# Two of three branch projections as Strassen pairs in a hybrid decoder layer on one Trainium2 core

## The chip, the cores and the metric

The kernel runs on one core of a Trainium2 chip. The core's engines work side by side, each in its own order: TensorE (PE in the profile; its weight loads are PEld), VectorE (DVE), ScalarE (ACT), GpSimd (POOL) and SyncE (SP), and its DMA queues are fed by SP, POOL and ACT. The metric is the device time of one execution in microseconds, here the median of three runs.

## The reference

One mixer layer, for a prompt of 1024 tokens and 8 single-token samples, width D = 1024, all in float32:

```python
h = rmsnorm(x, norm_gain)
proj = h @ w_in                                # q, k, v, gla_g, a_lr, u, pool_g, xq, xg, merge
br_gla  = rmsnorm(gla(q, k, v, gate(a_lr)))    * silu(gla_g)
br_pool = multiscale_pool(u)                   * silu(pool_g)
br_x    = cross_attention(xq, memory)          * silu(xg)
bproj   = einsum('btnw,nwd->btnd', [br_gla, br_pool, br_x], w_branch)   # three 1024 x 1024 products
merged  = sum over n of sigmoid(merge[n]) * bproj[n]
y = rmsnorm(x + merged @ w_out)
```

The change concerns `bproj` and `merged`: three products of a [1024 x 1024] weight with a branch's [1032 tokens x 1024] output (1024 prompt tokens and 8 sample tokens), each multiplied by its gate, then summed.

## The kernel before, in words

All values lie with the channels on the 128 partitions and the 1032 tokens along the free dimension, in two halves of HT = 516, each taken in two pieces of QT = 258. A product in float32 is made of three matmuls on values split into a high and a low part (`mm3`, lines 240 to 242: high times high, low times high, high times low). `split` (lines 221 and 222; with a scale lines 224 and 225) makes the parts: ACT copies the high one, then DVE subtracts it to get the low one.

**The input projection** is a list of 40 `Pair`s (0 to 39), each 256 columns of `w_in`. A pair uses one level of Strassen's method (Winograd's form): the weights are cut into four blocks, and the tokens and input channels of h too; seven products of a combined weight block with a combined block of h replace eight. The weight combinations are made for each pair (`operands`: four DVE additions at line 301, seven splits) three products ahead (`AHEAD = 3`) of their use. The seven combinations of h ("11", "21", "t2", "t1", "t3", "22", "t4", the order of `RIGHT`) are made once, and their split parts stay in 28 of the 30 large tiles of the pool `E` (1032 elements); the other two hold a pair's results c1 and c2.

Product (i, j) is the j-th of pair i. The sequence `seq` runs (i,1), (i,2), (i,3), (i,4), (i+1,0), (i,5), (i,6). A product is 24 matmuls of 258 columns. ACT copies accumulators aside (`saved`, line 612), DVE adds pieces: line 677 after product 1, line 694 after product 4, line 703 after product 5. `finish` then sends the result to scratch memory on POOL's queue. Pairs 0 to 15 make q, k, v and so on, 16 to 27 the merge gates, 28 to 39 the branches' SiLU gates, each multiplied (lines 636 and 638) by the branch's own result, which `mixed` loads (`mix` tiles) into the ring `R` of 15 small tiles. Attention, gated linear attention and pooling run in between, up to pair 36.

**The plain stage** follows: 24 units, one for 128 columns of `w_branch` in one branch (cross, then gated linear attention, then pool: `ORDER = (2, 0, 1)`). A unit is 72 matmuls of 384 or 264 columns over 8 tiles `bh`, `bl`, which `branch_k` loads and splits. At its end DVE multiplies by the sigmoid of the merge gate (line 1508) and adds the sum so far from scratch (line 1510), and the sum goes back to scratch or, in the last branch, becomes the split operand `mg` of the output projection, which is the last stage.

PE and SP keep the order in which the program issues their work; on DVE, ACT and POOL a scheduler sets it from data dependencies and from orders written with `issue_after`. SP's queue takes loads strictly in turn: a load that waits for its tile holds those behind it.

Of the kernel before, what the change touches and what calls it, by code (L numbers as in the profile page):

```python
# [42 lines left out]
EW = 1032  # L43
EXP_LN_SET = 6
# [3 lines left out]
def trunk_kernel(ctx: ExitStack, tc: tile.TileContext,  # L48
# [65 lines left out]
    def R(shape, dt=F32, name="r"):  # L114

        return shaped(wk.tile([P, 512], dt, tag="ring", name=name, bufs=NR), shape)

    def V(shape, dt=F32, name="v"):
        return shaped(wk.tile([P, 512], dt, tag="own", name=name, bufs=4), shape)
# [68 lines left out]
    brs = [cp.tile([P, NK, NS], F32, name=f"brs{n}") for n in range(3)]  # L188
# [13 lines left out]
    acc_scr = [scratch(NK, f"acc{n}_", (P, TT)) for n in range(2)]  # L202
# [78 lines left out]
    ORDER = (2, 0, 1)  # L281

    class Pair:


        def __init__(self, src, dst, s0=None, gated=None, turned=False):
            self.src, self.dst, self.s0, self.gated, self.raw = src, dst, s0, gated, [None, None]
            self.turned = turned
# [300 lines left out]
    def operand(name, k, src):  # L589
        hi, lo = (E([2, HT], F32R, name=f"o{name}{k}{j}") for j in range(2))  # L590
        split(hi, lo, src)
        ops.setdefault(name, []).append((hi, lo))
# [12 lines left out]
    def run_product(n):  # L605
# [18 lines left out]
        def finish(t, e):  # L624
# [3 lines left out]
            if p.gated:  # L628
# [11 lines left out]
                nc.vector.tensor_tensor(t[:, :, 512:HT], t[:, :, 512:HT], ss, op=ALU.mult)  # L640
            if p.turned:
# [24 lines left out]

        if j == 0:
# [13 lines left out]
        elif j == 2:  # L681
            p.r2 = []
            for c in product(p.x, n, False):
                p.r2.append(saved(p.x, c, "r2"))
                yield
# [5 lines left out]
        elif j == 4:  # L691
            for c in product(p.x, n, False):
# [6 lines left out]
        elif j == 5:  # L699
            p.e2 = E([2, HT], name="c2")  # L700
            mixed(1)
            for c in product(p.z, n, False):
# [4 lines left out]
        else:  # L707
            for c in product(p.x, n, False):
# [92 lines left out]
    def cross_scaled(h):  # L801
        xs = wk.tile([P, 16], F32, tag="xsq", name="xsq", bufs=2).rearrange("p (i b) -> p i b", i=2)
# [528 lines left out]
    def emit(n, ahead=AHEAD):  # L1331
        prepare(n + ahead)
        if seq[n] == (28, 0):
# [102 lines left out]
    units = [(o, n, d) for o, n in enumerate(ORDER) for d in range(NK)]  # L1436
    inputs = {}

    def fetch(u):
# [10 lines left out]
        acc = None  # L1450
        if o > 0:
            acc = E([TT], name="acc")
            nc.sync.dma_start(out=acc, in_=acc_scr[o - 1][d])
        inputs[u] = w, sig, acc
# [9 lines left out]
    br.append(branch_k(ORDER[0], 7))  # L1464
# [29 lines left out]
    for u, (o, n, d) in enumerate(units):  # L1494
        if d == 0 and o:
# [3 lines left out]
        w, sig, acc = inputs.pop(u)  # L1499
        act(sig, sig, AF.Sigmoid)  # L1500
        ts = [PX() for _ in CH]
# [54 lines left out]
    for hf, order in enumerate(ORDERS):  # L1556
        for tb in order:
# [13 lines left out]
            if hf == 0:  # L1571
                x = (E([D], name="y") if tb < 8 else RAW("ys").rearrange("p a b -> p (a b)"))[:m]
                nc.sync.dma_start(out=x, in_=x_p[tb * P:(tb + 1) * P] if tb < 8 else x_s)
                rows_[tb], sums[tb] = x, wk.tile([P, 4], F32, tag="yq", name="yq", bufs=9)[:m]
# [69 lines left out]
```

## Time and profile before

| | |
|---|---|
| Median of 3 runs | 1431.19 us (1431.14 to 1432.55) |
| The profiled execution, in all | 1428.62 us |
| Its span, first to last instruction | 1426.9 us |
| Granted TensorE clock | 0.998 of full |
| PE busy | 1403.6 us (98%) |
| DVE busy | 919.8 us (64%) |
| ACT busy | 678.3 us (48%) |
| The last gated pairs without other work on PE | 20.16 us each |
| Plain stage, 24 units | 1054.40 to 1326.37 us |
| From the end of the plain stage to the end of the span | 100.5 us |

A row of groups reads: source line, engine, operation, output tile <- input tiles (with partitions x elements), count, busy time and mean ns of one, and the idle time of the engine before them with what ended it. A row of a timeline reads: start, length (both us), the instruction, and the idle time before it in brackets. Lines such as L222 are those of the kernel before; in the changed kernel the same statements stand a few lines lower (L222 is L224, L677 is L768, L694 is L787, L703 is L797).

### The profile page before, as it was taken

How to read it: one execution, taken by the hardware profiler on the slowest of the kernel's cores; microseconds unless marked ns; L12 is line 12 of the kernel's file. 1: busy time of each engine (PE TensorE's matmuls, PEld its weight loads, DVE VectorE, ACT ScalarE, POOL GpSimd, SP SyncE). 2: the span in 40 equal slices, each digit the busy share in tenths (PEclk: the TensorE clock that was granted, in tenths of full speed). 3: DMA queues.
4: the chain of work that ended last, by engine and by line, in shares of the span. 5: the costliest groups of instructions: out<-in, count | busy, mean ns of one | idle time of the engine just before them, and what ended most of it. 6: DMA issues, size and time to landing. Idle time of an engine off the chain costs nothing.

```text
span 1426.9 us, 28403 instructions
## 1 busy us (share of the span) xinstructions
PE 1403.6 (98%) x10625; PEld 1345.0 (94%) x10625; DVE 919.8 (64%) x2108; ACT 678.3 (48%) x1582; POOL 293.6 (21%) x529
## 2 busy tenths in 40 slices
PE   7999999999899999999999999999999999999998
PEld 6899999999899999999999999999999999999876
DVE  6956766857687777767765777876662534654336
ACT  6744434534566656656554545444472422333222
POOL 4154222336442222222221111110000000000000
PEclk9999999999999999999999999999999999999999
DMA  9367786877564565545444556476484687632633
GB/s 347 117 202 248 251 280 208 258 222 237 138 190 130 170 192 163 165 152 166 155 150 146 176 162 210 150 217 204 150 263 148 225 273 232 228 105 86 227 112 117
DMA packets 194197, 270.05 MB, mean 189 GB/s; under 512 B 24252, under 2 KB 144084, under 8 KB 194052
## 3 DMA queue, kind: packets, MB, share of 16 engines
q1 hardware_dynamic: 129692, 151.36, 34.1%
q0 software_dynamic: 26208, 78.94, 15.5%
q10 hardware_dynamic: 38160, 37.95, 9.6%
q8 instruction: 83, 1.36, 0.4%
q14 instruction: 54, 0.44, 0.1%
HBM read 185.84 MB, written 82.80 MB: 188 GB/s over the span
## 4 chain that ended last, share of the span: by engine, by line
PE 92%; DMA 4%; DVE 3%; ACT 1%; issue 1%; SPq 0%; POOL 0%; ACTq 0%; DVEq 0%
PE px L240 26%; PE px L241 26%; PE px L242 26%; PE pz L241 2%; PE pz L242 2%; PE pz L240 2%; DMA raw<-in_w_in_dram 2%; PE pz L461 1%; PE pz L1040 1%; PE pz L1019 1%; DMA qb<-xqs 1%; PE pz L867 1%; PE pz L1021 1%; DMA pT<-pts 0%; PE pz L1126 0%
## 5 line engine op out<-in xcount | busy, mean ns | idle before, releaser
L240 PE MATMUL px<-bh,wbh 128*128 128x384 f32 (+1 forms) x576 | 184.3, 320 | 0.0
L241 PE MATMUL px<-bl,wbh 128*128 128x384 f32 (+1 forms) x576 | 184.0, 319 | 0.0
L242 PE MATMUL px<-bh,wbl 128*128 128x384 f32 (+1 forms) x576 | 183.8, 319 | 0.0
L612 ACT ACTIVATE r<-px 128x258 f32<-128x258 f32 x240 | 90.1, 377 | 54.4 <-PE px L242 53.5
L241 PEld LDWEIGHTS px<-bl,wbh 128*128 128x128 f32 x576 | 108.3, 188 | 0.0
L242 PEld LDWEIGHTS px<-bh,wbl 128*128 128x128 f32 x576 | 108.3, 188 | 0.0
L240 PEld LDWEIGHTS px<-bh,wbh 128*128 128x128 f32 x576 | 108.3, 188 | 0.0
L240 PE MATMUL px<-o,a12h 128*128 128x258 f32 x320 | 92.0, 288 | 1.4 <-DVE c L703 1.4
L240 PE MATMUL px<-ot,s1h 128*128 128x258 f32 x320 | 93.3, 292 | 0.0
L240 PE MATMUL px<-o,s4h 128*128 128x258 f32 x320 | 92.3, 288 | 0.3 <-DVE c L694 0.3
L240 PE MATMUL px<-o,a11h 128*128 128x258 f32 x320 | 92.4, 289 | 0.0
L240 PE MATMUL px<-ot,s2h 128*128 128x258 f32 x320 | 92.3, 288 | 0.0
L240 PE MATMUL px<-ot,a22h 128*128 128x258 f32 x320 | 92.0, 288 | 0.0
L240 PE MATMUL px<-ot,s3h 128*128 128x258 f32 x320 | 91.9, 287 | 0.0
L241 PE MATMUL px<-ot,s2h 128*128 128x258 f32 x320 | 90.6, 283 | 0.5 <-DVE ot L222 0.5
L241 PE MATMUL px<-o,a11h 128*128 128x258 f32 x320 | 90.7, 283 | 0.3 <-DVE o L222 0.3
L241 PE MATMUL px<-o,s4h 128*128 128x258 f32 x320 | 90.7, 283 | 0.0
L242 PE MATMUL px<-o,a11l 128*128 128x258 f32 x320 | 90.7, 283 | 0.0
L242 PE MATMUL px<-o,s4l 128*128 128x258 f32 x320 | 90.7, 283 | 0.0
L242 PE MATMUL px<-ot,s3l 128*128 128x258 f32 x320 | 90.5, 283 | 0.0
L241 PE MATMUL px<-ot,a22h 128*128 128x258 f32 x320 | 90.4, 283 | 0.0
L242 PE MATMUL px<-ot,s1l 128*128 128x258 f32 x320 | 90.4, 282 | 0.0
(479 smaller groups left out, 4687.2 us busy)
## 6 DMA issues: line engine op xcount, KB each, us to landing
raw<-in_w_in_dram ACTq DMA_DIRECT2D x72, 512.0 KB, 4.1
msc<-c POOLq DMA_DIRECT2D x24, 516.0 KB, 4.6
brsc<-c POOLq DMA_DIRECT2D x24, 516.0 KB, 4.1
sig<-msc SPq DMA_DIRECT2D x24, 516.0 KB, 6.1
brr<-brsc SPq DMA_DIRECT2D x48, 256.0 KB, 5.5
wbr<-in_w_branch_dram SPq DMA_DIRECT2D x24, 512.0 KB, 5.9
acc<-sig POOLq DMA_DIRECT2D x16, 516.0 KB, 5.4
acc<-acc SPq DMA_DIRECT2D x16, 516.0 KB, 7.2
```

The lines of the kernel that those rows point to most:

```text
L240: nc.tensor.matmul(out, lhsT=lh, rhs=rh, start=start, stop=False, skip_group_check=more)
L241: nc.tensor.matmul(out, lhsT=lh, rhs=rl, start=False, stop=False, skip_group_check=more)
L242: nc.tensor.matmul(out, lhsT=ll, rhs=rh, start=False, stop=stop, skip_group_check=more)
L461: nc.tensor.matmul(t[:, :DV], lhsT=memT[k // 2][:, k % 2, a * P:(a + 1) * P], rhs=raw[k // 2][:, k % 2], start=k == 0, stop=k == NK - 1)
L612: nc.scalar.activation(r, acc[c][:, :QT], AF.Copy)
L867: nc.tensor.matmul(t[32 * j:32 * j + 32, :DV], lhsT=pm[:, a, 4 * i + j, :], rhs=vc[j][:, a, :], start=a == 0, stop=a == 1)
L1019: nc.tensor.matmul(t[0:64, 0:P], lhsT=ki[:, 0:64], rhs=qi, start=True, stop=True)
L1021: nc.tensor.transpose(t[:, P:2 * P], kt, ident)
L1040: nc.tensor.matmul(to, lhsT=kiqi[:, 1, cs], rhs=st, start=False, stop=True)
```

## The change

The projections of cross (n = 2) and pool (n = 1) become eight more pairs, 40 to 43 and 44 to 47. Their weights are columns of `w_branch`, and their right operands are the branch's output in place of h. The order is now `(2, 1, 0)`, one merge pair (the old pair 27) moves behind the gated ones to place 39, and the gated pairs move up by one (27 to 38).

The seven right operands change twice, at pair 39 (for cross) and at pair 43 (for pool). This turnover is spread over the products: four blocks of the branch's output come as 16 tiles `b` (12 of the ring `R`, 4 of `V`), DVE makes the four differences t1, t3, t2, t4 from them by 16 subtractions of 516 elements (line 623) during the pair before (38 and 42), and each of the seven is split when the old operand of the same name has been used for the last time. "11", "21" and "22" are loaded once more as wide tiles `x` (2 x 516) into freed `E` tiles. The ring's tiles grow from 512 to 516 elements.

A branch pair multiplies its results by the sigmoid of the merge gate, loaded as four tiles `sg` (line 717), and stores them in scratch, each branch by itself. The plain stage is left with the eight units of gated linear attention; each loads the two stored results, adds them, and adds its own product.

```diff
-    ORDER = (2, 0, 1)
+    ORDER = (2, 1, 0)
...
+    pairs.append(pairs.pop(27))
+    for o, n in enumerate(ORDER[:NBR]):
+        pairs += [Pair(w_branch[n][:, 2 * P * j:2 * P * (j + 1)], acc_scr[o][j], branch=(o, n, j)) for j in range(4)]
     NPAIR = len(pairs)
+    TURNS = {39 + 4 * o: ORDER[o] for o in range(NBR)}
...
+    def block_loaded(n, name, alloc):
+        r, c = int(name[0]) - 1, int(name[1]) - 1
+        turn[name] = [loaded(br_scr[n][2 * r + k // 2][:, 2 * (k % 2) + c], [HT], "b" + name, alloc) for k in range(4)]
+
+    def operand_loaded(n, name):
+        r, c = int(name[0]) - 1, int(name[1]) - 1
+        turn["x", name] = [loaded(br_scr[n][2 * r + k][:, c:4:2], [2, HT], "x" + name, E) for k in range(2)]
+
+    def operand_split(v, name):
+        for x in turn.pop(("x", name)):
+            wide = not isinstance(x, list)
+            hi = E([2, HT], F32R, name=f"v{name}h")
+            lo = x.bitcast(F32R) if wide else E([2, HT], F32R, name=f"v{name}l")
+            with tc.issue_after(last["hi"].ins), tc.issue_after(last["lo"].ins):
+                for y, h, l in [(x, hi, lo)] if wide else [(x[q], hi[:, q], lo[:, q]) for q in range(2)]:
+                    split(h, l, y)
+            ops.setdefault((v, name), []).append((hi, lo))
+
+    def difference(x, y, out, name):
+        with tc.issue_after(last["lo"].ins):
+            for k in range(4):
+                nc.vector.tensor_tensor(out[k], x[k], y[k], op=ALU.subtract)
+        turn["x", name] = [out[:2], out[2:]]
+
+    def turnover(i, j):
+        for at, n in TURNS.items():
+            v, step = 1 + list(TURNS).index(at), (i - at, j)
+            if step == (-2, 3):
+                block_loaded(n, "12", R)
+                block_loaded(n, "11", R)
+            elif step == (-1, 0):
+                block_loaded(n, "22", R)
+            elif step == (-2, 6):
+                block_loaded(n, "21", V)
+            elif step == (-1, 1):
+                difference(turn["12"], turn["11"], turn["11"], "t1")
+            elif step == (-1, 2):
+                difference(turn["22"], turn["12"], turn["12"], "t3")
+            elif step == (-1, 3):
+                difference(turn["22"], turn["11"], turn["22"], "t2")
+            elif step == (-1, 4):
+                difference(turn["21"], turn["22"], turn["21"], "t4")
+            elif step == (-1, 5):
+                operand_loaded(n, "11")
+            elif step == (0, 1):
+                operand_split(v, "11")
...
+            elif step == (1, 2):
+                operand_split(v, "t4")
...
             for k in range(4):
-                hi, lo = ops[RIGHT[j]][k // 2]
+                hi, lo = ops[version(i), RIGHT[j]][k // 2]
...
+            if p.branch:
+                for i, sg in enumerate(p.mix[e]):
+                    nc.vector.tensor_tensor(t[:, i], t[:, i], sg, op=ALU.mult)
...
-    units = [(o, n, d) for o, n in enumerate(ORDER) for d in range(NK)]
+    units = [(o, ORDER[o], d) for o in range(NBR, 3) for d in range(NK)]
...
+        for q, x in enumerate(more):
+            nc.vector.tensor_tensor(acc[:, q * HT:(q + 1) * HT], acc[:, q * HT:(q + 1) * HT], x, op=ALU.add)
```

The cut in `turnover` continues in the same way: x21 is loaded after (39,2), t2 split after (39,3), "21" after (39,4), t1 after (40,0), t3 after (39,5), x22 loaded after (39,6), and "22" split after (40,1).

**DVE around the last gated pair.** In the kernel before, between products 4 and 6 of the last gated pair but one, DVE has the weights' low parts (a12l, s2l, s1l), the sums of line 694 and 703, and the multiplies with `mix`:

```order
L222 TENSOR_TENSOR a22l<-raw,a22h 128x512
L694 TENSOR_TENSOR c_13990<-px,r_14101 128x258
L222 TENSOR_TENSOR a12l<-raw,a12h 128x512
L694 TENSOR_TENSOR c_13990<-px,r_14116 128x258
L638 TENSOR_TENSOR c_13990<-c_13990,mix 128x512
L640 TENSOR_TENSOR c_13990<-c_13990,brs_115 128x2x4
L222 TENSOR_TENSOR s2l<-ws,s2h 128x512
L703 TENSOR_TENSOR c_14168<-px,r_14034 128x258
L301 TENSOR_TENSOR ws<-raw,ws 128x512
L703 TENSOR_TENSOR c_14168<-px,r_14048 128x258
```

In the changed kernel the same stretch of pair 39 (`c_14812` and `c_15021` are its results; it has no `mix`) carries the low parts of the new operands "21" and t1 (the `x` and `vt1l` tiles):

```order
L787 TENSOR_TENSOR c_14812<-px,r_14955 128x258
L224 TENSOR_TENSOR x_14877<-x_14877,v21h 128x1032
L224 TENSOR_TENSOR x_14879<-x_14879,v21h 128x1032
L224 TENSOR_TENSOR a12l<-raw,a12h 128x512
L303 TENSOR_TENSOR ws<-ws,raw 128x512
L224 TENSOR_TENSOR vt1l<-b_14355,vt1h 128x516
L224 TENSOR_TENSOR vt1l<-b_14357,vt1h 128x516
L224 TENSOR_TENSOR vt1l<-b_14359,vt1h 128x516
L224 TENSOR_TENSOR vt1l<-b_14361,vt1h 128x516
L224 TENSOR_TENSOR s2l<-ws,s2h 128x512
L797 TENSOR_TENSOR c_15021<-px,r_14861 128x258
L797 TENSOR_TENSOR c_15021<-px,r_14875 128x258
```

Between line 787 and line 797, two wide and four middle subtractions now stand; the first line 797 moved behind them.

**SP at the same place.** The loads of the `x` tiles stand in SP's order behind the last four `mix` loads of the gated pairs, and ahead of the first gate rows `sg`:

```order
L823 DMA mix<-mixsc_3_185 128x512 x4
L823 DMA x_14764<-brsc_0_214 128x2x516
L823 DMA x_14766<-brsc_1_215 128x2x516
L823 DMA x_14877<-brsc_2_216 128x2x516
L823 DMA x_14879<-brsc_3_217 128x2x516
L823 DMA x_15091<-brsc_2_216 128x2x516
L823 DMA x_15093<-brsc_3_217 128x2x516
L823 DMA sg<-msc_0_202 128x516 x4
```

In the kernel before, the loads of the plain stage's operands (`brr`, `brs`) stand there. At the second turnover the `x` loads stand between gate rows in the same way.

More of the change, by code (lines that the diff above doesn't have):

```diff
@@ L114, in R @@
     def R(shape, dt=F32, name="r"):
-        return shaped(wk.tile([P, 512], dt, tag="ring", name=name, bufs=NR), shape)
+        return shaped(wk.tile([P, HT], dt, tag="ring", name=name, bufs=NR), shape)
     def V(shape, dt=F32, name="v"):
-        return shaped(wk.tile([P, 512], dt, tag="own", name=name, bufs=4), shape)
+        return shaped(wk.tile([P, HT], dt, tag="own", name=name, bufs=4), shape)
     def WS(shape, name="ws"):
@@ L187, in trunk_kernel @@
     smp = cp.tile([P, 32 * NS], F32, name="smp")
-    brs = [cp.tile([P, NK, NS], F32, name=f"brs{n}") for n in range(3)]
+    brs = [cp.tile([P, NK, NS], F32, name=f"brs{n}") if n != 1 else smp[:, :NK * NS].rearrange("p (k b) -> p k b", k=NK)
+           for n in range(3)]
     als = cp.tile([P, NS], F32, name="als")
@@ L201, in trunk_kernel @@
     pt_scr = scratch(4 * NH, "pts", (8, 32, 4, 64))
-    acc_scr = [scratch(NK, f"acc{n}_", (P, TT)) for n in range(2)]
+    acc_scr = [scratch(4, f"acc{n}_", PAIR) for n in range(2)]
     mkv_scr = [scratch(NH, f"mkvs{o}", (P, 2, DV)) for o in range(2)]
@@ L591, in operand @@
         split(hi, lo, src)
-        ops.setdefault(name, []).append((hi, lo))
+        ops.setdefault((0, name), []).append((hi, lo))
+    turn = {}
+    def block_loaded(n, name, alloc):
[4 more added lines that the diff above has]
+        turn["x", name] = [loaded(br_scr[n][2 * r + k][:, c:4:2], [2, HT], "x" + name, E) for k in range(2)]
@@ L595, in product, with version @@
+    def version(i):
+        return pairs[i].branch[0] + 1 if pairs[i].branch else 0
     def product(acc, n, start):
@@ L665, in mixed, with factors, sigmoids @@
                     p.mix[e].append(loaded(src, [512], "mix"))
+        def factors(e):
+            if p.branch:
+                o, n, g = p.branch
+                for i in range(2):
+                    row = (0, 3, 1, 2)[2 * e + i]
+                    p.mix[e].append(loaded(m_scr[n][g][:, row], [HT], "sg"))
+        def sigmoids(e):
+            if p.branch:
+                for sg in p.mix[e]:
+                    with tc.issue_after(last["hi"].ins):
+                        act(sg, sg, AF.Sigmoid)
         if j == 0:
@@ L1449, in fetch @@
         nc.sync.dma_start(out=sig.rearrange("p (h t) -> p h t", h=2), in_=m_scr[n][d // 2][:, 2 * (d % 2):2 * (d % 2) + 2])
[L1450 to L1454, printed above, removed]
+        acc = E([TT], name="acc")
+        nc.sync.dma_start(out=acc.rearrange("p (h t) -> p h t", h=2),
+                          in_=acc_scr[o - 1][d // 2][:, 2 * (d % 2):2 * (d % 2) + 2])
+        more = [loaded(acc_scr[0][d // 2][:, 2 * (d % 2) + q], [HT], "acm") for q in range(2)] if NBR == 2 else []
+        inputs[u] = w, sig, acc, more
     br = []
@@ L1463, in trunk_kernel @@
         emit(n)
-    br.append(branch_k(ORDER[0], 7))
+        turnover(*seq[n])
+    br.append(branch_k(ORDER[NBR], 7))
     mg, late = [None] * NK, []
@@ L1494, in trunk_kernel @@
     for u, (o, n, d) in enumerate(units):
-        if d == 0 and o:
+        if d == 0 and o > NBR:
             br = [branch_k(n, k) for k in range(NK)]
@@ L1498, in trunk_kernel @@
             fetch(u + 1)
-        w, sig, acc = inputs.pop(u)
+        w, sig, acc, more = inputs.pop(u)
         act(sig, sig, AF.Sigmoid)
+        for q, x in enumerate(more):
+            nc.vector.tensor_tensor(acc[:, q * HT:(q + 1) * HT], acc[:, q * HT:(q + 1) * HT], x, op=ALU.add)
         ts = [PX() for _ in CH]
@@ L1573, in trunk_kernel @@
                 nc.sync.dma_start(out=x, in_=x_p[tb * P:(tb + 1) * P] if tb < 8 else x_s)
-                rows_[tb], sums[tb] = x, wk.tile([P, 4], F32, tag="yq", name="yq", bufs=9)[:m]
+                rows_[tb], sums[tb] = x, smp[:m, 64 + 4 * tb:68 + 4 * tb]
             x, sq = rows_[tb], sums[tb]
```

35 lines of the change are left out of this document (27 added, 8 removed).

## The prediction

> **What bounds the kernel now.** I read the page first (engine shares, the chain that ended last), then TensorE's waits, then the two stages that the change touches, by time windows and instruction by instruction.
>
> ```profile
> span 1426.9 us, 28403 instructions
> PE 1403.6 (98%) x10625; PEld 1345.0 (94%) x10625; DVE 919.8 (64%) x2108; ACT 678.3 (48%) x1582; POOL 293.6 (21%) x529
> PE 92%; DMA 4%; DVE 3%; ACT 1%; issue 1%; SPq 0%; POOL 0%; ACTq 0%; DVEq 0%
> ```
>
> TensorE (PE) is busy 98% of the span and is 92% of the chain. Its waits (who waited, for whom, us in total, times, longest) are small, and those that name the projection (px) tell where VectorE (DVE) can hurt:
>
> ```profile
> PE px L240 <- DVE c L703: 1.4, 1, 1.4
> PE px L240 <- DVE c L694: 0.3, 1, 0.3
> ```
>
> L694 and L703 read accumulators that a later product needs again: L694 reads z before product 5 adds to it, and L703 reads z, whose bank the next pair's product 1 takes. A late DVE stalls TensorE at these two points.
>
> The two stages, by windows that begin at the first matmul of a pair's product 1 and of a plain unit group (columns: length, busy us and count of each engine, clock, DMA share, GB/s), with the rows that set the cuts:
>
> ```profile
> 996.27 0.28 PE L240 MATMUL px<-o,a12h 128*128 128x258 f32 x1
> 1016.43 0.28 PE L240 MATMUL px<-o,a12h 128*128 128x258 f32 x1
> 1054.40 0.34 PE L240 MATMUL px<-bh,wbh 128*128 128x384 f32 x1
> 1326.37 0.39 PE L240 MATMUL px<-woh,mg0h 128*128 128x512 f32 x1
> 996.27:1016.43 20.16, 20.16 (x171) 20.16 (x169) 12.37 (x23) 8.76 (x18) 1.28 (x2) 1.00 0.52 158
> 1036.59:1054.40 17.81, 17.52 (x146) 17.32 (x145) 14.12 (x32) 14.70 (x29) 0.90 (x3) 1.00 0.80 249
> 1054.40:1145.21 90.81, 90.81 (x578) 90.81 (x577) 37.13 (x73) 34.65 (x59) 5.02 (x9) 1.00 0.65 207
> 1145.21:1235.77 90.56, 90.56 (x579) 90.56 (x577) 40.59 (x86) 27.96 (x48) 4.26 (x8) 1.00 0.70 229
> 1235.77:1326.37 90.60, 90.60 (x578) 90.60 (x577) 42.05 (x74) 27.43 (x35) 3.48 (x8) 1.00 0.43 138
> ```
>
> A Strassen pair (256 output columns) takes 20.16 us, eight plain units (128 columns each) 90.6 to 90.8 us, all with PE full and the clock at 1.00. DVE is at 61% in the pair and 41 to 46% in the plain stage.
>
> **The change part by part.** *TensorE.* The plain units of two branches go: 90.81 + 90.60 = 181.4 us (the branch left takes the row of 90.56). Eight pairs of the same shape come: 8 x 20.16 = 161.3 us. The difference is 20.1 us off a full engine. In matmuls, 168 per pair at 20.16 / 168 = 120 ns against 72 per unit at 11.33 / 72 = 157 ns.
>
> [...]
>
> *VectorE.* The trace gives both how long an instruction lasts and how close the next starts:
>
> ```profile
> 1014.30 0.69 DVE L222 TENSOR_TENSOR s1l<-ws,s1h 128x512 fp32r<-128x512 f32 x1
> 1014.91 0.68 DVE L638 TENSOR_TENSOR c<-c,mix 128x512 f32<-128x512 f32 x1
> 1015.51 0.68 DVE L301 TENSOR_TENSOR ws<-raw 128x512 f32<-128x512 f32 x1
> 1012.49 0.42 DVE L703 TENSOR_TENSOR c<-px,r 128x258 f32<-128x258 f32 x1
> 1012.82 0.68 DVE L301 TENSOR_TENSOR ws<-raw,ws 128x512 f32<-128x512 f32 x1
> 1018.38 0.16 DVE L640 TENSOR_TENSOR c<-c,brs 128x8 f32<-128x8 f32 x1
> 1018.46 0.42 DVE L677 TENSOR_TENSOR c<-px,r 128x258 f32<-128x258 f32 x1
> L222 DVE TENSOR_TENSOR mg0l<-sig,mg0h x1: 1234/1234/1234, 1250.8 to 1250.8; 128x1032 fp32r<-128x1032 f32 x1
> ```
>
> An instruction on 512 elements lasts 0.69 us, but the next starts after 0.605; on 258 it is 0.42 and 0.33, on 8 0.08 to the next. For 1032 (1.23 us) I take 1.15 by the same overlap. The second number is what a queue of ready work costs.
>
> Each turnover (the new operands for one branch) falls on three pairs. By DVE's order in the changed kernel, in rows between two L768 groups:
> - pair before the last old one (38): 29 wide rows (16 of them the new differences), 6 of 258, 2 tiny (0.08): 29 x 0.605 + 6 x 0.33 + 0.2 = 19.7 us.
> - last old pair (39): 23 wide, 4 of 1032, 6 of 258: 13.9 + 4.6 + 2.0 = 20.5.
> - first new pair (40): 21 wide, 2 of 1032, 6 of 258: 12.7 + 2.3 + 2.0 = 17.0.
>
> 57.2 us in 60.5 of TensorE: the first turnover fits, with nothing to spare. The second (pairs 42, 43, 44) has four gate multiplies (L717) in pair 43, which pair 39 lacks: 19.5 + 22.9 + 16.4 = 58.8, and at the end of pair 43 DVE stands 42.4 - 40.3 = **2.1 us** behind, just where L797 (the old L703) must free z for product 1 of pair 44. I charge these 2.1. By the full durations the first two pairs would be 22.9 + 23.3 = 46.2 (5.9 over) and 22.5 + 26.1 = 48.6 (8.3 over): 14.2 us for both. So DVE's bounds are 0 and 14.2; the starts in a full queue are the nearer row. It has been full before at little cost: while the last pair of the kernel before prepares the plain stage, DVE is busy 10.68 of 11.56 us (the first row below), and PE loses this:
>
> ```profile
> 1038.70:1050.26 11.56, 11.27 (x94) 11.06 (x93) 10.68 (x24) 10.21 (x23) 0.90 (x3) 1.00 0.69 220
> 1049.41 0.28 PE L242 MATMUL px<-o,s4l 128*128 128x258 f32 x1
> 1049.98 0.39 PE L240 MATMUL px<-o,s4h 128*128 128x258 f32 x1 [0.29 <-DVE c L694]
> ```
>
> that is, 0.57 us between two starts where 0.12 is usual.
>
> [...]
>
> *ScalarE (ACT)* gets the high halves (0.52 apart on 512), with six of 1032 a turnover:
>
> ```profile
> 1044.88 1.14 ACT L221 ACTIVATE bh<-brr 128x512 fp32r<-128x512 f32 x2
> 1045.92 0.19 ACT L221 ACTIVATE bh<-brs 128x8 fp32r<-128x8 f32 x1
> L221 ACT ACTIVATE mg0h<-sig x1: 1069/1069/1069, 1249.7 to 1249.7; 128x1032 fp32r<-128x1032 f32 x1
> ```
>
> Pair 43, the fullest: 23 wide x 0.52 + 4 x 1.0 + 8 small x 0.3 = 18.4 us of 20.16. It is behind DVE there, not ahead; I charge nothing, and if its cover goes it is DVE's price again, since each low half waits for its high one.
>
> *Transfers.* A turnover loads 16 blocks of 264 KB and six of 528 KB: 7.4 MB, most of it within three pairs, where the weights, results and gate rows move some 156 GB/s more (1 MB each in 20 us): (7.4 + 9.4) MB / 60 us = 280 GB/s. The window of 249 GB/s above already has a DMA share of 0.80, and transfers there land later than usual (page, then the same view from 1030 to 1056):
>
> ```profile
> raw<-in_w_in_dram ACTq DMA_DIRECT2D x72, 512.0 KB, 4.1
> sig<-msc SPq DMA_DIRECT2D x24, 516.0 KB, 6.1
> ...
> sig<-msc SPq DMA_DIRECT2D x4, 516.0 KB, 7.6
> wbr<-in_w_branch_dram SPq DMA_DIRECT2D x4, 512.0 KB, 6.2
> ...
> DVE ws L301 <- DMA raw<-in_w_in_dram: 26.2, 19, 3.4
> ```
>
> DVE waits for weights (raw) already now, 1.4 us a time, because the second half of a pair's weights is asked for only when the s3 subtraction frees a buffer. In a turnover such a wait is not covered by slack. At 6.2 instead of 4.1 it is 2.1 us later, of which I count 0.6 covered: **1.5 us per turnover, 3.0 for both** (bounds 0 and 2 x 3.4).
>
> *The rest.* 16 adds of stored sums (wide) in the plain stage, 9.7 us of DVE: hidden, as DVE is busy 40.59 of 90.56 us there; uncovered it would be 9.7. Moving one merge pair behind the gated ones swaps equal pairs: 0. The last pair before the plain stage has gate multiplies where it had mix multiplies: 0.
>
> Sum: -20.1 + 2.1 + 3.0 = -15.0 us: span 1426.9 - 15.0 = 1411.9. That profiled execution took 1428.6 us in all, the median of the three runs is 1431.2; applied to the median: **1416.2 us**.
>
> **The rivals.**
> 1. *DVE binds by full durations* (its waits on ACT leave no overlap): the turnovers lose 14.2 instead of 5.1: 1431.2 - 20.1 + 14.2 = 1425.3. For it: each low half waits for a high half. Against: the starts 0.605 apart. Chance 0.13.
> 2. *Slower: operands arrive late.* The x tiles can be loaded only into room that the old operand's last product frees; SyncE's (SP) queue issues them behind mix and gate rows, which wait for DVE:
>
> ```profile
> SPq L728 <- DVE c L638: 18.9, 6, 4.2
> SPq L728 <- DVE c L640: 41.0, 9, 8.3
> ```
>
> From an operand's last old product to its first new one lie six products, 6 x 2.88 = 17.3 us. Needed: 0.8 to issue, 7.6 to land, 2.1 and 1.2 to split: 11.7. It decides when SP is held more than 5.6 us at each; with three operands in each of two turnovers it costs 6 x (hold - 5.6), and the kernel is slower from a hold of 9 us on. At 10.4: 1431.2 - 20.1 + 28.8 = 1439.9. Against: the longest such holds, 4.2 and 8.3, are once each. Chance 0.08.
> 3. *Columns save nothing*: were the new matmuls to pay the plain 157 ns, 1344 of them take 211.7 us instead of 181.4: 1461.5. The row of 20.16 speaks against it. [...] Chance 0.01.
> 4. *The saving isn't there*: the last gain is taken by the changed edge to the plain stage, 1431. PE's order has exactly the 192 more, shorter matmuls: chance 0.02.
>
> **How the numbers follow.** Forecast 0.76, rivals 0.13, 0.08, 0.01, 0.02. A difference under about 0.2% (2.9 us) can't be told from none; so slower begins at 1434.1 and faster ends at 1428.3. Faster: 0.76 + 0.09 of rival 1 = 0.85. Same: 0.04 of rival 1, 0.02 of rival 2, 0.02: 0.08. Slower: 0.06 + 0.01 = 0.07. The forecast's own range goes from no stall at all (1411.1, and 0.6 for the gap at 1049 that may go) to DVE and weights at twice my charge, 1421.3; the range that holds eight in ten runs from 1410.5 to 1426, which takes in rival 1.
>
> **What would show it.** Windows over pairs 41, 45 and 46 at 20.16 us with PE full; over pairs 38 to 40 at 60.5 to 63, over 42 to 44 at 62 to 65. PE's waits there name L797 or L787, and DVE is above 90% busy in pairs 39 and 43; plain units stay at 11.3. DVE waits for raw rise by one or two of 2 us per turnover. Wrong: PE waits on x or v tiles (rival 2), more than 7 us lost in either turnover (rival 1), pairs off 20.16 (rival 3), or a plain stage longer than 91 us (rival 4).

## The result, and the profile after

| | before | changed |
|---|---|---|
| Median (first comparison) | 1431.16 us (1429.60 to 1432.55, 4 runs) | 1416.69 us (1412.39 to 1418.71, 4 runs) |
| The profiled execution, in all | 1428.62 us | 1417.57 us |
| Its span | 1426.9 us | 1415.9 us |

The ratio of the times is 0.990, with a 95% interval of 0.9884 to 0.9916. The kernel is 14.5 us faster by the medians; forecast were 15.0 (1416.2 us). Two later comparisons of the same pair gave 0.9891 (0.9870 to 0.9911) and 0.9919 (0.9896 to 0.9941), by the medians 15.9 and 11.3 us.

The page of the changed kernel: its span, the engines' busy times and the chain that ended last.

```profile
span 1415.9 us, 29040 instructions
PE 1390.2 (98%) x10817; PEld 1330.9 (94%) x10817; DVE 997.1 (70%) x2216; ACT 717.9 (51%) x1680; POOL 298.9 (21%) x529
PE 88%; DMA 6%; DVE 3%; issue 1%; ACT 1%; POOL 0%; SPq 0%; DVEq 0%; ACTq 0%
```

PE has 192 more matmuls and is busy 13.4 us less; DVE has 77 us more. PE's share of the chain falls from 92% to 88%, and what takes its place is mostly DMA (4 to 6%). PE's waits in the same profile (who waited, for whom, us in total, times, longest):

```profile
PE pz L953 <- DVE ps L942: 5.5, 2, 3.1
PE px L242 <- DVE c L797: 0.4, 1, 0.4
PE px L242 <- DVE c L787: 0.2, 1, 0.2
```

The two waits that the prediction watched, for z at L787 and L797, are down to 0.6 us in the whole program (before: 0.3 and 1.4). The wait for `ps`, the probabilities of the sample attention, was 2.5 us before and is 5.5. That is far ahead of the change.

Cutting the two spans at product 1 of pair 39 (1036.59 before, 1044.33 after) and at the first matmul of the output projection (1326.37 and 1314.31) shows where the time went:

| | before | changed | difference |
|---|---|---|---|
| start to pair 39 | 1036.59 | 1044.33 | +7.7 |
| pair 39 to the output projection | 289.78 | 269.98 | -19.8 |
| output projection to the end | 100.5 | 101.5 | +1.0 |

So in this profile the change brought nearly all of its 20.1 us, and 7.7 us were lost in a part that it hardly touches. Another 1.0 went behind the plain stage, and this part recurs: from the output projection to the end both profiles of the kernel before take 100.5 us, the three of the changed kernel 101.5, 101.2 and 101.8. Windows over the changed kernel's pairs 39, 41 and 44 and its eight plain units (length, busy us and count of PE, PEld, DVE, ACT, POOL, then clock, DMA share, GB/s):

```profile
1044.33:1064.46 20.13, 20.13 (x170) 20.13 (x169) 17.50 (x29) 15.51 (x30) 1.28 (x2) 1.00 0.46 161
1084.68:1104.83 20.15, 20.15 (x170) 20.15 (x169) 12.75 (x23) 8.83 (x19) 1.28 (x2) 1.00 0.76 265
1145.15:1165.74 20.59, 20.44 (x170) 20.24 (x169) 20.16 (x36) 14.44 (x30) 1.28 (x2) 1.00 0.89 305
1223.96:1314.31 90.35, 90.35 (x578) 90.35 (x577) 52.90 (x93) 31.91 (x44) 3.85 (x8) 1.00 0.60 197
```

The Strassen pairs on a branch take 20.15 to 20.22 us, the plain units 11.3 each. Only pair 44 is clearly longer, by 0.43 us over 20.16. Without any stall the stretch from pair 39 to the plain units would take 8 x 20.16 + 17.81 = 179.1 us; it took 179.6.

**Where the 7.7 us went.** By the starts of the pairs, the changed kernel is 0.8 us later at pair 3, 4.7 at pair 4, 7.7 at pair 6, and 6.6 to 7.8 later at every pair from there to pair 39. DVE, first before, then changed (start, length, instruction, idle time before it):

```profile
156.25 0.69 DVE L301 TENSOR_TENSOR ws<-raw 128x512 f32<-128x512 f32 x1 [3.44 <-DMA raw<-in_w_in_dram]
157.04 0.34 DVE L847 TENSOR_SCALAR ps<-ps,sm 8x256 f32<-8x256 f32 x1
```
```profile
158.48 0.69 DVE L303 TENSOR_TENSOR ws<-raw 128x512 f32<-128x512 f32 x1 [3.25 <-DMA raw<-in_w_in_dram]
159.26 0.34 DVE L942 TENSOR_SCALAR ps<-ps,sm 8x256 f32<-8x256 f32 x1
```

In both, DVE stands at a weight sum until raw weights land, and the small instruction that makes `ps` stands behind it. PE, in its fixed order, transposes `ps` next. Before, it idled 1.63 us for that; in the changed kernel, 3.15:

```profile
157.52 0.26 PE L858 MATMUL pz<-ident,ps 8*128 8x8 f32 x2 [1.63 <-DVE ps L847]
```
```profile
159.75 0.35 PE L953 MATMUL pz<-ident,ps 8*128 8x8 f32 x2 [3.15 <-DVE ps L942]
```

Meanwhile its clock fell. The windows (the column of 1.00 is the granted clock) before, and changed:

```profile
156.00:159.00 3.00, 1.48 (x12) 1.49 (x13) 1.73 (x5) 0.93 (x5) 0.00 (x0) 1.00 0.30 105
159.00:162.00 3.00, 3.00 (x28) 3.00 (x26) 2.81 (x8) 2.50 (x7) 1.02 (x2) 1.00 0.01 3
```
```profile
156.00:159.00 3.00, 0.60 (x6) 0.40 (x4) 0.52 (x1) 0.00 (x0) 0.00 (x0) 0.91 0.83 287
159.00:162.00 3.00, 2.25 (x11) 2.26 (x12) 1.78 (x7) 1.70 (x6) 0.00 (x0) 0.50 0.01 4
162.00:165.00 3.00, 3.00 (x16) 3.00 (x16) 2.97 (x7) 1.27 (x3) 1.79 (x4) 0.50 0.14 25
```

At 0.50 PE does 16 matmuls in 3 us, where it did 28. The pair with the wait of 3.15 us took 34.5 us, where it took 30.7 before with the wait of 1.63 in it, so wait and clock together cost some 5.5. The same happens once more at 223 us (a wait of 2.34, and a clock of 0.50 up to 226.7).

### The profile page after: what moved, and what is told of

It reads as the page before. It is cut to its first block, busy times and chain, and to the rows that moved or that the text cites. A ratio compares the mean times of both kernels' runs of the same rounds, so it can differ in the third digit from the quotient of the medians.

```text
span 1415.9 us, 29040 instructions
## 1 busy us (share of the span) xinstructions
PE 1390.2 (98%) x10817; PEld 1330.9 (94%) x10817; DVE 997.1 (70%) x2216; ACT 717.9 (51%) x1680; POOL 298.9 (21%) x529
## 4 chain that ended last, share of the span: by engine, by line
PE 88%; DMA 6%; DVE 3%; issue 1%; ACT 1%; POOL 0%; SPq 0%; DVEq 0%; ACTq 0%
PE px L242 25%; PE px L243 25%; PE px L244 25%; PE pz L243 2%; PE pz L244 2%; PE pz L242 2%; DMA raw<-in_w_in_dram 2%; PE pz L1135 1%; PE pz L1114 1%; DMA wm<-in_w_mv_dram 1%; DMA qb<-xqs 1%; PE pz L962 1%; PE pz L1116 1%; DMA x<-brsc 1%; PE pz L467 0%
## 5 line engine op out<-in xcount | busy, mean ns | idle before, releaser
L686 ACT ACTIVATE r<-px 128x258 f32<-128x258 f32 x288 | 107.7, 377 | 62.4 <-PE px L244 58.1
L242 PE MATMUL px<-ot,s1h 128*128 128x258 f32 x320 | 94.0, 294 | 0.0
L303 DVE TENSOR_TENSOR ws<-raw 128x512 f32<-128x512 f32 x96 | 65.8, 686 | 39.1 <-DMA raw<-in_w_in_dram 27.7
L242 PE MATMUL px<-o,a12h 128*128 128x258 f32 x320 | 92.0, 288 | 0.4 <-DVE c L797 0.4
L242 PE MATMUL px<-ot,s3h 128*128 128x258 f32 x320 | 92.3, 288 | 0.0
L243 PE MATMUL px<-ot,s1h 128*128 128x258 f32 x320 | 91.0, 285 | 0.0
L243 PE MATMUL px<-ot,s3h 128*128 128x258 f32 x320 | 90.7, 284 | 0.0
L244 PE MATMUL px<-ot,a22l 128*128 128x258 f32 x320 | 90.4, 283 | 0.0
L243 PE MATMUL px<-o,a12h 128*128 128x258 f32 x320 | 90.4, 282 | 0.0
L244 PE MATMUL px<-ot,s2l 128*128 128x258 f32 x320 | 90.3, 282 | 0.0
```

Source lines behind the costliest of these rows:

```text
L242: nc.tensor.matmul(out, lhsT=lh, rhs=rh, start=start, stop=False, skip_group_check=more)
L243: nc.tensor.matmul(out, lhsT=lh, rhs=rl, start=False, stop=False, skip_group_check=more)
L244: nc.tensor.matmul(out, lhsT=ll, rhs=rh, start=False, stop=stop, skip_group_check=more)
L303: nc.vector.tensor_tensor(s, x, y, op=op)
L686: nc.scalar.activation(r, acc[c][:, :QT], AF.Copy)
```

## The experiments

The questions were two: is the early loss caused by the change, and what do the turnovers cost, and why? Up to pair 24 the engines' orders of the two kernels are the same but for one DVE instruction (`xsq`, a scaling of 16 columns), which moved because its tile has one buffer now instead of two.

### The changed kernel once more

No edit.

> The changed kernel once more, nothing edited. In its first profile pair 4 begins 4.66 us and pair 7 begins 7.73 us later than before (265.87 against 258.14 us), although up to there the two programs differ by one DVE instruction's place (xsq). Theory A, that instruction is the cause: the second profile shows pair 7 at 265.9 again, give or take 1 us, and the median stays at 1416.7. Theory B, the transfers of that stage land by chance and the wait for ps with the halved clock behind it comes and goes: pair 7 begins somewhere between 258 and 266 us, with another sum of waits for ps (5.5 us in the first profile), and single runs spread by 5 us and more (1412 to 1419).

Measured: 1414.9 us (1411.77 to 1421.32, 6 runs), ratio 0.9891. In its profile pair 7 begins at 257.83 us, 0.3 us earlier than before, and the waits at the places of question are these:

```profile
PE px L242 <- DVE c L787: 2.2, 5, 1.2
PE pz L953 <- DVE ps L942: 1.7, 2, 1.1
PE px L242 <- DVE c L797: 1.4, 2, 1.1
```

Theory B: the same program loses 7.7 us there in one execution and nothing in another. The turnovers, however, which had cost 0.5 us, now cost 3.7 (182.8 us from pair 39 to the plain units). Pairs 39, 41 and 44 of this profile:

```profile
1038.23:1059.85 21.62, 20.43 (x171) 20.23 (x169) 17.50 (x29) 15.51 (x30) 1.28 (x2) 1.00 0.45 154
1080.05:1100.92 20.87, 20.46 (x170) 20.25 (x169) 12.69 (x23) 8.71 (x19) 1.28 (x2) 1.00 0.76 265
1141.67:1162.85 21.18, 20.67 (x171) 20.26 (x169) 20.76 (x37) 14.70 (x30) 1.28 (x2) 1.00 0.89 299
```

Pair 39 is 1.49 us longer than in the first profile with the same DVE work in it. The difference stands in one row of DVE, the first profile's and then this one's:

```profile
1053.84 0.69 DVE L303 TENSOR_TENSOR ws<-raw 128x512 f32<-128x512 f32 x1 [2.63 <-DMA raw<-in_w_branch_dram]
```
```profile
1049.22 0.69 DVE L303 TENSOR_TENSOR ws<-raw 128x512 f32<-128x512 f32 x1 [4.12 <-DMA raw<-in_w_branch_dram]
```

DVE waited 4.12 us for weights instead of 2.63, 1.49 more, and the pair grew by just that, at L787. So 2.6 us of such a wait are covered in pair 39, and each microsecond more is paid in full.

### The moved instruction alone

```diff
-        xs = wk.tile([P, 16], F32, tag="xsq", name="xsq", bufs=2)
+        xs = wk.tile([P, 16], F32, tag="xsq", name="xsq", bufs=1)
```

(in the kernel before)

> The kernel before with one edit: xsq has one buffer instead of two, so that DVE's order up to pair 24 is the changed kernel's. Theory A (this instruction costs the 7.7 us ahead of pair 7): 1438 to 1439 us, pair 7 at 265 to 266 us. Theory B (chance): 1430 to 1433 us, no difference that can be told, pair 7 within 3 us of 258.1 unless the wait for ps with the halved clock shows in the same profile.

Measured: 1432.08 us (1426.97 to 1435.84, 12 runs) beside 1430.77 for the kernel before, ratio 0.9997 (0.9982 to 1.0013). So the instruction's place costs at most 1.9 us, by the interval; it is not the 7.7. The profile shows what chance does in a kernel without the change: pair 7 begins 3.6 us late, with 4.6 us of waits for `ps` (the longest, 2.5 at 158 us, with the clock still at 1.00 behind it; the other, 2.2 at 219 us, with a clock of 0.50).

### The sample softmax scaled on ACT

```diff
         act(p, t[:NS, :NM], AF.Exp, bias=nm, accum_out=sm)
-        nc.vector.reciprocal(sm, sm)
-        nc.vector.tensor_scalar(p, p, sm, None, op0=ALU.mult)
+        act(sm, sm, AF.Ln)
+        nc.scalar.activation(sm, sm, AF.Identity, scale=-1.0, bias=nm)
+        act(p, t[:NS, :NM], AF.Exp, bias=sm)
```

> The changed kernel with the sample softmax scaled on ACT (a second Exp with the logarithm of the sum in its bias) instead of DVE's reciprocal and multiply, so that ps no longer stands behind the weight sum that waits for raw. If the loss ahead of pair 7 is that wait and the clock behind it: PE's waits for ps go from 5.5 us to under 0.5, the clock stays at 1.00 from 150 to 250 us, pair 7 begins at 256 to 259 us and the median is 1408 to 1411. Rival: PE stops a little later for something else that is queued behind the same late weights on DVE (pm, pT, the sums of a pair), and the median stays within 2 us of 1416.7.

> The kernel before with the same edit of the sample softmax. Its profile waits 2.5 us for ps and keeps its clock: 1428 to 1430 us. If the change itself is worth the 20.1 us of TensorE and costs nothing ahead of it, this kernel stands 19 to 21 us above the changed kernel with the same edit; if the changed kernel has a loss of its own ahead of pair 7 that the edit does not touch, by 12 to 14 us only.

Measured: on the changed kernel 1413.73 us (1409.82 to 1413.93, 4 runs), ratio 0.9868 (0.9851 to 0.9885); on the kernel before 1430.53 us, ratio 0.9999 (0.9986 to 1.0013). In the changed kernel's profile the waits at that place are

```profile
PE pz L242 <- ACT p L76: 1.3, 1, 1.3
PE pz L954 <- ACT ps L76: 0.6, 1, 0.6
```

and pair 7 begins at 258.54 us. Waits for `ps` are gone but for 0.6 us; the time is above the 1408 to 1411 expected, and this profile's turnovers lost 4.4 us (pair 43 alone took 22.52 us, with a wait of 2.53 us for weights). Beside the changed kernel of the same comparison (1414.9) the edit gains 1.2 us by the medians and some 3 by the ratios, whose intervals overlap, so that a gain is not shown. On the kernel before the edit gains nothing: there its profile has a wait of 2.2 us for `p` and 1.1 for `ps`, and pair 7 at 260.75, so the stall only moved. The two kernels with the edit stand 16.8 us apart by their medians and 18.7 by their ratios, between the 12 to 14 and the 19 to 21 that were set against each other and nearer to the second. In their profiles, which lie 16.7 us apart, the changed kernel reaches pair 39 1.7 us earlier, so no loss of its own shows ahead of it there; what is missing from 20.1 are the 4.4 us of the turnovers and 0.9 behind the plain stage.

### Twice the differences

```diff
                 nc.vector.tensor_tensor(out[k], x[k], y[k], op=ALU.subtract)
+                nc.vector.tensor_tensor(out[k], out[k], out[k], op=ALU.max)
```

> The changed kernel with 16 more DVE instructions of 516 elements in each turnover (each difference is followed by a maximum of the result with itself), so 9.7 us more by starts 0.605 apart, 11.0 by durations. From product 1 of pair 39 to the plain stage the two profiles of the changed kernel take 179.6 and 182.8 us, where no stall at all would make 179.1. Theory: DVE's price is the spacing, and what is over its room stops TensorE: the first turnover then needs 57.2 + 9.7 = 66.9 us in 60.5, the second 58.8 + 9.7 = 68.5: 6.4 and 8.0 us lost and a little of late weights, the stage 193 to 197 us, the kernel 1429 to 1433 us. Rival, full durations: DVE was over its room already and each added instruction costs 0.69 us: 22 us, 1437. Rival, DVE has slack and only late weights ever cost: under 3 us, 1418.

Measured: 1432.68 us (1427.89 to 1438.21, 10 runs), ratio 1.0014 (0.9996 to 1.0032): the whole gain is eaten by 32 instructions. The time is in the range of the first theory, but the place is another, and the stage from pair 39 on takes 190.8 us, under its 193 to 197. The profile is that of the longest run, 1438.21 us. Pairs 38 and 42:

```profile
1024.73:1052.43 27.70, 22.61 (x170) 22.44 (x169) 26.96 (x49) 6.85 (x15) 1.28 (x2) 0.88 0.43 133
1113.89:1141.67 27.78, 22.28 (x171) 22.10 (x170) 26.64 (x47) 6.74 (x15) 1.28 (x2) 0.88 0.44 143
```

and PE's waits from pair 38 to the plain units:

```profile
PE px L242 <- DVE c L788: 11.3, 4, 5.5
```

The pair with the differences pays at once (7.5 and 7.6 us); pairs 39 to 41 together only 1.0, pair 44 3.0. The room of 17.0 us of work in 20.16 of pair 40 does not help pair 38, since the sums that free z stand in DVE's order behind the added work of their own pair: the first of them (L788) begins 19.05 us into pair 38, where it began at 11.78 in the changed kernel, and PE asks for it some 14.5 us into the pair. And of the 7.5 us only some 5.1 are wait: 2.4 are PE's busy time, 22.61 instead of 20.16, at a mean clock of 0.88.

### One branch instead of two

```diff
-NBR = 2
+NBR = 1
```

> The changed kernel with one branch (cross) as Strassen pairs and two in the plain stage: one turnover, four pairs. If the gain is TensorE's columns less a small price per turnover: 10.05 us less than before and 0.3 to 2.5 us of stall, 1421 to 1424 us. If the first turnover were the dear one and the second free, as the raw waits of pairs 39 and 41 might say: 1424. If the gain were in something else than the columns (the shorter plain stage, the order of branches), not near the half: under 1418 or over 1427.

Measured: 1422.39 us (1422.17 to 1426.22, 4 runs), ratio 0.9942 (0.9924 to 0.9960). That is 8.6 us by the medians, where half the columns are 10.05 and the one turnover lost 0.6 in its profile. Its pairs 39 to 42 take 20.22, 20.22, 20.64 and 20.15 us.

### The differences on GpSimd

```diff
-        with tc.issue_after(last["lo"].ins):
-            for k in range(4):
-                nc.vector.tensor_tensor(out[k], x[k], y[k], op=ALU.subtract)
+        for k in range(4):
+            nc.gpsimd.tensor_tensor(out[k], x[k], y[k], op=ALU.subtract)
```

> The changed kernel with the 32 differences on GpSimd instead of DVE, which gets 9.7 us of room back in each turnover. If the stalls of the turnovers (0.5 and 3.7 us in two profiles) are DVE's backlog, the stage from pair 39 to the plain units takes 179.1 to 179.8 us. If they are late weights, TensorE still stops in pairs 39 or 41 behind DVE's wait for raw and only pairs 43 and 44 lose their share: 180.5 to 182. Rival, GpSimd is too slow or its stores are held up by the differences: waits for vt tiles, the stage over 186 us. Median: 1412 to 1415 for the first two, over 1418 for the last.

Measured: 1419.71 us (1418.56 to 1423.86, 4 runs), ratio 0.9926 (0.9905 to 0.9948), so not better than the changed kernel. Pairs 39, 40 and 43 take 20.13, 20.18 and 20.35 us, pair 41 27.31. There POOL, whose differences had waited 16 us for their blocks, runs several in a row (first fence), and DVE beside it (second fence) does this:

```profile
1077.44 4.85 POOL L622 TENSOR_TENSOR b<-b,b 128x516 f32<-128x516 f32 x3 [0.88 <-DMA b<-brsc]
1082.98 7.49 POOL L622 TENSOR_TENSOR b<-b,b 128x516 f32<-128x516 f32 x6
```
```profile
1079.34 1.79 DVE L303 TENSOR_TENSOR ws<-raw 128x512 f32<-128x512 f32 x1
1081.06 1.79 DVE L303 TENSOR_TENSOR ws<-raw,ws 128x512 f32<-128x512 f32 x1
1082.77 8.26 DVE L716 TENSOR_TENSOR c<-c,sg 128x516 f32<-128x516 f32 x1
```

A DVE instruction of 0.69 us takes 1.79, and one takes 8.26, as long as POOL's six differences. The work left DVE, but beside those six differences DVE got through one instruction. The stage from pair 39 on takes 186.5 us, as long as the last rival had it, but by another wait: PE stands 4.7 us for a low part of the weights (s3l) that DVE made too late.

### A fourth buffer for raw weights

```diff
-NR = 15
+NR = 13
...
-        return wk.tile([P, 4, CT], F32, tag="raw", name=name, bufs=3)
+        return wk.tile([P, 4, CT], F32, tag="raw", name=name, bufs=4)
```

> The changed kernel with four buffers for raw weights instead of three (the ring R gives two of its 15 tiles), so that the second half of a pair's weights is asked for earlier than the s3 subtraction. If late weights make the stalls of the turnovers: DVE's waits for raw between pairs 38 and 47 fall from some 10 us to under 3, and the stage from pair 39 to the plain units takes 179.1 to 180.5 us. If DVE's backlog makes them, the waits for raw fall as well but the stage stays at 181.5 to 183. The rest of the program has the same buffer and a smaller ring, so its median is not read for this; 1408 to 1420.

Measured: 1451.32 us, ratio 1.0129 (1.0107 to 1.0151). It settles nothing of its question. DVE still waits 13.9 us for weights in that stretch, since the load keeps its place in ACT's order behind the high half of s3, so a free buffer is not used earlier; and the ring of 13 brings stalls of its own (the pairs from 39 on take 194.2 us, and pair 39 begins 13.8 us later than in the changed kernel's first profile). What it shows is only that two tiles of the ring are worth more here than a raw buffer.

### The x21 tiles behind the weights

In the profile of the second measurement the late weights of pair 39 are asked for at the same moment as two tiles of 516 KB (ACT's queue, then SP's; the KB of the profile are 1024 bytes):

```profile
1040.38 0.37 ACTq L294 DMA_DIRECT2D raw<-in_w_branch_dram  x1
```
```profile
1040.46 1.18 SPq L823 DMA_DIRECT2D x<-brsc  x2
```

DVE can use them 8.8 us later, where the median of raw to landing is some 4.

```diff
+        if name == "21":
+            turn["x", name] = [E([2, HT], name="x" + name) for k in range(2)]
+            for k, x in enumerate(turn["x", name]):
+                with tc.issue_after(last["raw"].ins):
+                    nc.scalar.dma_start(out=x, in_=br_scr[n][2 * r + k][:, c:4:2])
+            return
```

> The changed kernel with the two x21 tiles of each turnover loaded on ACT's queue behind the second half of the next pair's weights, instead of on SP's at the same moment (1040.46 and 1040.38 us in the second profile). Theory: the stalls of pairs 39 and 43 (1.5 and 0.4 us there, 0.6 and 2.4 in the profile with the softmax on ACT) come from these two transfers sharing the DMA engines: the raw weights then land in 4 to 5 us instead of 8.8, DVE's wait for them in pairs 39 and 43 stays under 1 us, and both pairs take 20.15 to 20.4 us. Pair 41, whose late weights meet other loads (b and sg tiles), is not helped: 20.2 to 20.9. Rival, DVE's own backlog: DVE waits less for raw, and the pairs stop as long as before. Rival, x21 itself now comes late: PE waits for v21 in pairs 40 and 44, over 21.5 us each. Median 1412 to 1416.

Measured: 1417.0 us (1415.34 to 1417.53, 4 runs), ratio 0.9903 (0.9886 to 0.9919), the same as the changed kernel and above the 1412 to 1416 expected. In its profile pairs 39, 41, 43 and 44 are

```profile
1041.24:1061.37 20.13, 20.13 (x170) 20.13 (x169) 18.18 (x30) 14.30 (x27) 1.28 (x2) 1.00 0.60 190
1081.54:1101.73 20.19, 20.19 (x170) 20.19 (x169) 14.09 (x25) 9.72 (x21) 1.28 (x2) 1.00 0.76 247
1121.92:1142.10 20.18, 20.18 (x171) 20.18 (x170) 18.93 (x31) 15.54 (x30) 1.28 (x2) 1.00 0.78 245
1142.10:1162.83 20.73, 20.41 (x171) 20.21 (x170) 19.78 (x35) 15.49 (x31) 1.28 (x2) 1.00 0.94 315
```

The turnovers cost 0.6 us in all. The waits for raw in pairs 39 and 43 are still 1.95 and 1.25 us (under 1 was expected), but the first is below the 2.6 that pair 39 covers. The weights of pair 39 take 6.7 us to land (1043.38 to 1050.06) although x21 is asked for only at 1047.20, so the two tiles explain a part of the lateness, and what makes the rest is open. The first profile of the changed kernel lost as little without the edit; one profile cannot show that the edit did it. What this profile gains there it lost early, with one wait of 3.2 us for `ps`.

### Both edits, beside the changed kernel

> The changed kernel with both edits, the sample softmax scaled on ACT and x21 behind the weights on ACT's queue. If each takes the share that its profile shows (some 2 us of waits for ps and of halved clock, some 1 to 2 us of the turnovers): 1410 to 1413 us, 2 to 5 us below the changed kernel in the same call. Rival, the early stage's stalls only change places: no difference from the changed kernel that can be told.

> The changed kernel, nothing edited, on the chip of the two others: 1413 to 1417 us. Its third profile: pair 7 begins anywhere from 257 to 266 us, the stage from pair 39 to the plain units takes 179.5 to 184 us, with the raw weights of pair 39 landing 7 to 9 us after they are asked for.

Measured side by side: both edits 1411.68 us (1409.21 to 1414.08, 4 runs), ratio 0.9868 (0.9849 to 0.9886); the changed kernel without them 1419.83 us (1413.76 to 1422.56, 6 runs), ratio 0.9919 (0.9896 to 0.9941). With both, pair 7 begins at 258.17 us and the turnovers cost 0.6 us; without, pair 7 begins at 266.08 and they cost 1.9. The intervals do not meet, so both edits together gain, by 8.2 us here where 2 to 5 were expected; the changed kernel beside them was above its 1413 to 1417. The edit of the softmax alone has the same ratio, 0.9868, so what the x21 edit adds to it is not shown. Both versions are 1.3% under the kernel before.

### The kernel before once more

> The kernel before once more, nothing edited, for a second profile of its early stage. If waits for ps and the halved clock come and go by the landing of transfers in any kernel: pair 7 begins at 258 to 266 us, later wherever PE waits for ps longer than the 2.5 us of the first profile, and not later where it waits less. If they belong to the changed kernel: 258.1, give or take 0.5 us. Time 1427 to 1435 us.

Measured: 1430.97 us, ratio 1.0007 (0.9991 to 1.0023). Pair 7 begins at 259.46 us, 1.3 late, with 2.4 us of waits for `ps` (the longest 1.8), about those of the first profile. Yet behind the longer one, of 1.75 us, its clock falls as well:

```profile
157.51 0.26 PE L858 MATMUL pz<-ident,ps 8*128 8x8 f32 x2 [1.75 <-DVE ps L847]
```
```profile
156.00:158.00 2.00, 0.49 (x4) 0.50 (x5) 1.73 (x5) 0.00 (x0) 0.00 (x0) 1.00 0.51 179
158.00:160.00 2.00, 2.00 (x14) 2.00 (x13) 0.82 (x4) 1.94 (x7) 0.00 (x0) 0.65 0.01 5
160.00:162.00 2.00, 2.00 (x11) 2.00 (x11) 2.00 (x5) 0.91 (x2) 1.04 (x2) 0.50 0.01 4
```

So the unedited kernel before has the clock's fall behind this stage too, in one execution and not in another.

## Why the prediction was right, and where its sum was not

The forecast was 1416.2 us, and 1416.69 was measured. The total came out by two errors of opposite sign, so that it came so near is luck: over all runs here the changed kernel averages 1417.3 us (16 runs) and the kernel before 1430.8 (68 runs), 13.5 us apart.

**TensorE's 20.1 us** held. Pairs on a branch take 20.15 to 20.22 us where little stops them, plain units 11.3, and one branch alone brings 8.6 us. The rival of columns that save nothing is out by the same rows.

**DVE's price is the spacing**, as taken: four of the new differences in a row take 2.51 us, that is 3 x 0.605 + 0.69, not 4 x 0.69.

```profile
1029.91 2.51 DVE L623 TENSOR_TENSOR b<-b,b 128x516 f32<-128x516 f32 x4
```

So the rival of full durations falls.

DVE's sums were right too. From the first L768 of a pair to that of the next DVE is busy as follows (first profile: pairs 38, 39 and 40, then 42, 43 and 44; length, DVE, clock, DMA share, GB/s), against 19.7, 20.5 and 17.0 and then 19.5, 22.9 and 16.4 in the prediction.

```profile
1026.22:1046.36 20.14, 19.77 (x39) 1.00 0.55 182
1046.36:1069.56 23.20, 20.57 (x34) 1.00 0.61 194
1069.56:1089.37 19.81, 17.34 (x31) 1.00 0.89 317
1108.56:1128.57 20.01, 19.65 (x35) 1.00 0.56 182
1128.57:1151.48 22.91, 22.91 (x39) 1.00 0.84 273
1151.48:1170.16 18.68, 16.72 (x29) 1.00 0.89 298
```

**The step "2.1 us behind at the end of pair 43"** had the wrong price: it charged being late one for one. DVE was late, and more than forecast: L768 begins 2.0 us into a pair as a rule, in pair 40 at 5.1 and in pair 44 at 6.3, which is 3.1 and 4.3 us late. Yet pairs 39 and 43 took 20.13 and 20.17 us, and pair 44 is 0.4 to 1.0 us over 20.16 in the three profiles of the changed kernel. PE does not ask for all of DVE's work, only for single results. The row of L797 that must free z for pair 44 begins 21.0 us after the start of pair 43 in the first profile (first row below), 4.8 later than in pair 37, and PE waited for nothing at product 1. In the third profile it is 5.3 later, and PE waited 0.16 us there (second row); in the second 5.8 later, and PE waited 0.28. The first profile's whole loss in pair 44, and half of that in the other two, stands at L787 instead.

```profile
1145.97 0.75 DVE L797 TENSOR_TENSOR c<-px,r 128x258 f32<-128x258 f32 x2
1149.39 0.39 PE L242 MATMUL px<-v21h,a12h 128*128 128x258 f32 x1 [0.16 <-DVE c L797]
```

So work that stands behind the result that PE asks for can run over into the next pair; work ahead of it costs what exceeds the time in hand there, as with the doubled differences, which moved L788 itself. A sum over three pairs tells neither.

**The step "late raw weights, 1.5 us per turnover, 0.6 covered"** had the right mechanism and wrong sizes. Six profiles with the same pair 39 (three of the changed kernel, then those with the softmax on ACT, with x21 moved, and with both) show its cover:

| DVE's wait for raw in pair 39 (us) | 2.63 | 4.12 | 3.46 | 3.33 | 1.95 | 2.32 |
|---|---|---|---|---|---|---|
| length of pair 39 (us) | 20.13 | 21.62 | 20.93 | 20.78 | 20.13 | 20.13 |

The length is 20.13 plus what the wait has over 2.6 us. In pair 41, with 12.7 us of DVE work, a wait of 4.92 cost 0.1 and one of 5.50 cost 0.7, so some 5 are covered; in pair 43, where DVE is full, 0.70 cost 0.4 and 2.53 cost 2.4 (with x21 moved, 1.25 cost nothing). The cover is the time in hand ahead of the row of L787 in that pair: not one number, and in pair 41 less than the 7.4 us that DVE has free in the whole pair. The 0.6 of the prediction rested on no row. Its 6.2 us to landing was too low as well: in pair 39 DVE could use the late weights 7.4, 8.8 and 8.2 us after they were asked for. The stalls of both turnovers were charged at 5.1 us and were 0.5, 3.7 and 1.9 in the three profiles, by when the transfers landed.

**The step "the rest: 0"** failed. It spoke of the moved merge pair and of what comes behind it alone. The first profile of the changed kernel had lost 7.7 us ahead of pair 39, the second 1.6, the third 9.3, all against one profile of before, and each lost 0.7 to 1.3 us more behind the plain stage, for which no run here shows the cause. These losses made up for the stalls that were charged too high. In the first profile the early loss is mostly waits for `ps` and the halved clock with them; in the third such a wait, of 3.03 us, brought about half of it, and 4.5 us were lost by pair 3, ahead of that wait, with a clock of 0.50 from 37.2 to 40.6 us. The change's own part in them is not the moved `xsq`, beyond 1.9 us. They come and go in the same program, and smaller ones, 1.3 us with a halved clock in the unedited kernel before and 3.6 in that with the moved `xsq`, were there without the change. Whether the changed kernel meets them more often than the kernel before stays open. Its three profiles lost 7.7, -0.3 and 7.9 us by pair 7. Four more runs, whose instructions on PE and DVE come in the same order up to there, lost 7.6 (doubled differences), 4.2 (one branch), 3.2 (x21 moved) and 0.5 (GpSimd). The two of before lost 0 and 1.3. This points to the changed kernel, but two profiles are too few to compare with, and the edit of the softmax gave some 3 us by the ratios on the changed kernel (their intervals overlap) and nothing on the one before.

**The other signs.** Pairs 38 to 40 took 60.5 us in the first profile and 62.0 in the second, as said (60.5 to 63); 42 to 44 took 60.9 and 61.9, under the 62 to 65 forecast. DVE is over 90% busy in pair 43, but at 87% in pair 39, where the wait for weights stands. Its waits for raw in the first turnover were 2.6 and 4.1 us in the first profile and 4.1 and 5.5 in the second, where one or two of 2 us were said. No wait of PE on `x` or `v` tiles as such appears (rival 2), though the loads of x21 stand beside the late weights of pair 39 and may have made a part of their delay.

## What to carry to other kernels

A wait on an engine that feeds TensorE costs only what makes a result later than TensorE asks for it: take from the profile when each such result is ready and when it is asked for, since the engine's busy time, pooled over a stretch or taken pair by pair, shows neither (here 2.6 us of DVE's wait in pair 39 cost nothing). A forecast whose total is right can hide two errors, so cut both spans at the change's first and last instruction before judging it, and profile the same program again before explaining a few microseconds. Where PE's fixed order meets a small result that stands behind a DMA-bound instruction on another engine, the stall can cost most of its length again in clock (here 3.15 us of wait and, as an estimate from the 5.5 us of both, some 2.3 of clock), or nothing (2.47 us at a clock of 1.00).

## What was not expected of the hardware

- **The clock after a short stop.** Waits of PE of 3.15, 2.34 and 1.75 us came with a granted clock of 0.50; one of 1.63 us at the place of the 1.75, one of 2.06 (one branch, at 221 us) and one of 2.47 (the kernel before with the moved `xsq`, at 158 us) did not, so the length of a stop alone does not decide it. In the first profiles of the two kernels every stretch at 0.50, but for the last of each trace, lasts 3.41 or 6.83 us (changed: from 158.49 to 165.32, from 223.34 to 226.75 and from 370.11 to 376.94; before: from 365.11 to 368.52). Why the 1.75 lost its clock and the 2.47 did not, no run here shows; the 1.75 was PE's only stop from 150 to 160 us (8.25 of the 10 us busy).
- **DVE beside GpSimd.** While POOL subtracts tiles, DVE instructions with two inputs that last 0.69 us elsewhere take 1.55 to 1.79, and one takes 8.26, beside six of POOL's that take 7.49 together (all in the run with the differences on GpSimd).
- **Landing times.** The same load of 512 KB lands after some 4 us as a rule and is used after 7.4 to 8.8 where two loads of 516 KB start beside it (6.7 and 7.1 where these start 3.8 us later). The spread within 7.4 to 8.8 alone moves pair 39 by up to 1.5 us from one execution to the next.
